# Fixed address phases for the operands of split fp32 matmuls in a two-layer decoder trunk

## The chip, the cores and the metric

The kernel runs on one core of a Trainium2 chip. The metric is the device time of one execution in microseconds (us), the median of several runs. The span of the profiled execution, from its first to its last instruction, is a little shorter than its device time.

## The reference

The reference computes a causal decoder trunk of two layers on one sequence of 256 tokens with 2,048 features, all in float32. Cut to what matters:

```python
for i in range(DEPTH):                       # 2 layers
    xn = rms_norm(x, norm_mix[i])
    y = nsa_mixer(xn, ...) if i % 2 == 0 else mlstm_mixer(xn, ...)
    x = x + y
    x = x + conv_glu_ffn(rms_norm(x, norm_ffn[i]), ...)
return rms_norm(x, norm_final)

def conv_glu_ffn(xn, w_up, conv_w, conv_b, w_down):
    u = xn @ w_up                            # 2048 -> 2 * 5632
    c = causal_conv_width_3(u, conv_w) + conv_b
    gate, val = c[..., :D_FF], c[..., D_FF:]
    return (silu(gate) * val) @ w_down       # 5632 -> 2048
```

The first mixer projects x to queries, keys, values and gates, attends over compressed blocks, selected blocks and a window, and projects back. The second is a matrix memory in chunks (mLSTM), with its own projections in and out. Most of the arithmetic lies in the dense projections: 2,048 by 11,264 up and 5,632 by 2,048 down in each layer, and the mixers' projections in and out.

## The kernel before

Every dense projection is made from split operands. A float32 tensor is held as two tensors of type fp32r, a high half and the rest, and a product is the sum of three matmuls: high by high, high by rest, rest by high. The weights come from HBM in pieces of 512 KB (`load_split`). SyncE's queue loads a piece into `raw` (four buffers), ACT copies it to the high half `whi` (line 188), DVE subtracts to get `wlo` (line 190); each of these has five buffers, used in turn. The activations' halves are `xh` and `xl` for the normed residual stream, `oh` and `ol` for what a mixer puts out (`moh` and `mol` in the second), and `gh` and `gl` for the gated FFN activations.

There are two kinds of product. A column product (`cols_times`, `cols_piece`, lines 224, 226, 227) gives 256 output features for all 256 tokens: weights are stationary (128 by 128), and a row of `xh` or `xl` moves (256 columns). For one contraction step kt there are six matmuls, three for each of two blocks of 128 features; four steps use one weight buffer, and 16 steps, 96 matmuls, make one product. Queries, keys, and the whole FFN up projection are made so. A row product (`rows_mm`, lines 196 to 198) gives 128 tokens by up to 512 features: a block of `xh`, `gh` or `oh` is stationary, and the weights move. `project_out` makes the out and down projections so, 12 matmuls of 512 columns for one weight buffer and one contraction step.

The order of the work is written out by hand. The FFN alternates an up stage of eight column products with a down stage. What follows a product on ACT and DVE is queued (`evacs`, `side`) and issued between weight pieces, so that TensorE always has the next piece's matmuls behind the present ones.

The tiles of a pool lie one behind another in each partition. The pools `const`, `main`, `wpool` and `small` come first, and each stage's pools after them. Before the change three kinds of tile are made longer than their contents by a constant, eight float32 elements, 32 bytes:

```python
SKEW = 8
xh = main.tile([P, KT, S + SKEW], F32R, name="xh")[:, :, :S]
hi = wpool.tile([P, 1024 + SKEW], F32R, name=nm("whi"), tag="whi", bufs=SPB)
gh = wk.tile([P, 8, S + SKEW], F32R, name=nm("gh"), tag="gh")[:, :, :S]
```

In the text, an operand's phase is its address in the partition modulo 256 bytes. `h`, the residual stream, starts at phase 32 and is 16,384 bytes long; `xh` lies behind it, then `xl`, then four buffers of `raw` with 4,096 bytes each, five of `whi`, five of `wlo`.

Of the kernel before, what the change touches and what calls it, by code (L numbers as in the profile page):

```python
# [12 lines left out]
F32 = mybir.dt.float32  # L13
F32R = mybir.dt.float32r
BF16 = mybir.dt.bfloat16
# [6 lines left out]
P = 128  # L22
D = 2048
KT = D // P
S = 256
# [8 lines left out]
EPS = 1e-6  # L34
QSCALE = float(np.float32(128 ** -0.5))
CAP = 15.0
SKEW = 8
NEG = -1e30

C_ID, C_MQ, C_MT, C_CA, C_C1, C_RP = 0, 0, 128, 256, 288, 320  # L40
# [23 lines left out]
def trunk(ctx: ExitStack, tc: tile.TileContext, x, positions, nsa_w_in, nsa_gate_b, nsa_cmp_pe,  # L64
# [3 lines left out]
    nc = tc.nc  # L68
# [4 lines left out]
    const = ctx.enter_context(tc.tile_pool(name="const", bufs=1))  # L73
    main = ctx.enter_context(tc.tile_pool(name="main", bufs=1))
    wpool = ctx.enter_context(tc.tile_pool(name="wpool", bufs=1))
    small = ctx.enter_context(tc.tile_pool(name="small", bufs=2))
    psum = ctx.enter_context(tc.tile_pool(name="psum", bufs=8, space=PSUM))

# [2 lines left out]
    def nm(s):  # L81
        uid[0] += 1
        return f"{s}_{uid[0]}"
# [4 lines left out]
    def fview(t):  # L88
        return t.bitcast(F32)

    h = main.tile([P, NT, D], F32, name="h")
    xh = main.tile([P, KT, S + SKEW], F32R, name="xh")[:, :, :S]
    xl = main.tile([P, KT, S + SKEW], F32R, name="xl")[:, :, :S]

    def load_x(pc):
        for t in range(NT):
# [18 lines left out]
    cst = const.tile([P, C_N - P], F32, name="cst")  # L115
# [1 line left out]

    ident_b = const.tile([P, P], BF16, name="ident_b")
    nc.gpsimd.tensor_copy(ident_b, ident)
    mq_b = const.tile([P, 2, P], BF16, name="mq_b")  # L120
    for b in range(2):
        nc.gpsimd.tensor_copy(mq_b[:, b, :], cst[:, C_MQ:C_MQ + P])
    mt_b = const.tile([P, 2, P], BF16, name="mt_b")
    for b in range(2):
        nc.gpsimd.tensor_copy(mt_b[:, b, :], cst[:, C_MT:C_MT + P])
    sel_b = const.tile([96, MH], BF16, name="sel_b")
    nc.gpsimd.tensor_copy(sel_b, cst[:96, C_SEL:C_SEL + MH])

# [16 lines left out]
    RAWB, SPB, PTB = 4, 5, 4  # L145
# [24 lines left out]
    def queued(engine):  # L170
        return tc.issue_after(fence[engine]) if engine in fence else nullcontext()
# [3 lines left out]
    def preload(w, k0, nk, c0, n):  # L175
        ready[w.tensor.name, w.offset, k0, c0] = load_split(w, k0, nk, c0, n)

    def load_split(w, k0, nk, c0, n):
        got = ready.pop((w.tensor.name, w.offset, k0, c0), None)
        if got is not None:  # L180
            return got
        view = lambda t: t[:, :nk * n].rearrange("p (k c) -> p k c", k=nk)
        raw = wpool.tile([P, 1024], F32, name=nm("raw"), tag="raw", bufs=RAWB)
        nc.sync.dma_start(view(raw), w[k0 * P:(k0 + nk) * P, c0:c0 + n].rearrange("(k p) c -> p k c", p=P))
        hi = wpool.tile([P, 1024 + SKEW], F32R, name=nm("whi"), tag="whi", bufs=SPB)
        lo = wpool.tile([P, 1024 + SKEW], F32R, name=nm("wlo"), tag="wlo", bufs=SPB)
        with queued("act"):
            latest["act"] = act(view(hi), view(raw), AF.Copy).ins  # L188
        with queued("ve"):
            latest["ve"] = ve.tensor_sub(view(lo), view(raw), fview(view(hi))).ins  # L190
        return view(hi), view(lo)
# [8 lines left out]
    def rows_times(w, c0, n, nk):  # L200
        accs = [bank() for _ in range(NT)]
        for k0 in range(0, KT, nk):
            m = min(nk, KT - k0)
            hi, lo = load_split(w, k0, m, c0, n)
            run_hooks()
            for i in range(m):
                kt = k0 + i
                for t in range(NT):
                    rows_mm(hi, lo, i, xh, xl, kt, t, accs[t][:, :n], 0, n, kt == 0, kt == KT - 1)
            tick()  # L210
        return accs
# [19 lines left out]
    def cols_times(w, c0):  # L231
        ps = pair_bank()
        for k0 in range(0, KT, 4):
            cols_piece(ps, w, c0, k0, 4)
        return ps
# [109 lines left out]
    def nsa(norm, nxt):  # L345
        with tc.tile_pool(name="nsa", bufs=1) as pool, tc.tile_pool(name="nsw", bufs=2) as wk:
# [55 lines left out]
            def rope(dst, src):  # L402
                shp = [32, 2, S]
                sw = wk.tile(shp, F32, name=nm("sw"), tag="sw", bufs=1)
                ve.stream_shuffle(sw, src, swap)
                ve.tensor_mul(sw, sw, sin[:, None, :].to_broadcast(shp))
                ve.tensor_mul(dst, src, cos[:, None, :].to_broadcast(shp))
                ve.tensor_add(dst, dst, sw)
# [91 lines left out]

            def q_out(pair, ps):
                qu = wk.tile([P, 2, S], F32, name=nm("qu"), tag="qu", bufs=3)
                qr = wk.tile([P, 2, S], F32, name=nm("qr"), tag="qr", bufs=2)
                ve.tensor_mul(qu, ps, rq[:, None, :].to_broadcast([P, 2, S]))
                act(qr, qu, AF.Copy)
                rope(qr[:32], qu[:32])
                q[pair] = (qu, qr)
# [158 lines left out]
            for pair in range(8):  # L666
                ps = cols_times(w, pair * 256)
                if pair == 1:
                    drain()
                    side.append(lambda: None)  # L670
                    side.extend(attention())
                evacs.append(partial(q_out, pair, ps))
            project_out(nsa_w_out[0], oh, ol, HEADS, nxt, gate_kt=12)

    def mlstm(norm, nxt):
        with tc.tile_pool(name="mls", bufs=1) as pool, tc.tile_pool(name="mlw", bufs=2) as wk:
# [4 lines left out]
            sog = pool.tile([P, NT, D], F32, name="sog")  # L681
            v1 = pool.tile([P, NT, MH, DV + 1], F32, name="v1")
            nc.gpsimd.memset(v1[:, :, :, DV:DV + 1], 1.0)
            oh = pool.tile([P, KT, S], F32R, name="moh")
            ol = pool.tile([P, KT, S], F32R, name="mol")
            gp = pool.tile([P, NT, 2 * MH], F32, name="gp")
# [164 lines left out]

    def ffn(layer, norm, nxt):
        with tc.tile_pool(name=f"ffn{layer}", bufs=1) as pool, tc.tile_pool(name=f"ffw{layer}", bufs=2) as wk:
            wu, wd = ffn_w_up[layer], ffn_w_down[layer]
            taps = tapc[:, layer]

            def conv(ff, tag, ps):
                uu = wk.tile([P, 2, S], F32, name=nm("u"), tag="u" + tag)
                ve.tensor_mul(uu, ps, norm.rbc2)  # L859
                ac = wk.tile([P, 2, S], F32, name=nm("ac"), tag="ac" + tag)  # L860
                for j in range(2):
                    f = ff + j
                    act(ac[:, j, :], uu[:, j, :], AF.Identity, bias=taps[:, 3, f:f + 1],  # L863
                        scale=taps[:, 2, f:f + 1])
                    ve.scalar_tensor_tensor(ac[:, j, 1:], uu[:, j, :S - 1], taps[:, 1, f:f + 1],  # L865
                                            ac[:, j, 1:], op0=ALU.mult, op1=ALU.add)
                    ve.scalar_tensor_tensor(ac[:, j, 2:], uu[:, j, :S - 2], taps[:, 0, f:f + 1],  # L867
                                            ac[:, j, 2:], op0=ALU.mult, op1=ALU.add)
                return ac

            groups = [list(range(0, 4))] + [list(range(f, f + 8)) for f in range(4, NFF, 8)]

            def up(ffs):
                gh = wk.tile([P, 8, S + SKEW], F32R, name=nm("gh"), tag="gh")[:, :, :S]
                gl = wk.tile([P, 8, S + SKEW], F32R, name=nm("gl"), tag="gl")[:, :, :S]
                for i in range(0, len(ffs), 2):
                    res = {}

                    def gate_out(ff, ps, res):
                        res["g"] = conv(ff, "g", ps)  # L880
                        act(res["g"], res["g"], AF.Silu)

                    def val_out(ff, ps, res, i):
                        va = conv(NFF + ff, "v", ps)
                        ve.tensor_mul(va, res["g"], va)
                        act(gh[:, i:i + 2, :], va, AF.Copy)
                        ve.tensor_sub(gl[:, i:i + 2, :], va, fview(gh[:, i:i + 2, :]))

                    evacs.append(partial(gate_out, ffs[i], cols_times(wu, ffs[i] * P), res))
                    evacs.append(partial(val_out, ffs[i], cols_times(wu, (NFF + ffs[i]) * P), res, i))  # L890
                return gh, gl

            def down(ffs, g, norm):
                n = len(ffs)
                project_out(wd[ffs[0] * P:(ffs[0] + n) * P, :], g[0], g[1], n, norm)

            prev = None
            for ffs in groups:
                g = up(ffs)
                if prev is not None:  # L900
                    down(*prev, None)
                prev = (ffs, g)
            down(*prev, nxt)
# [61 lines left out]
    after(12, n0.settle)  # L965
    nsa(n0, n1)
    ffn(0, n1, n2)
    mlstm(n2, n3)
    nf.load()
    ffn(1, n3, nf)  # L970


# [21 lines left out]
```

## Time and profile before

| | us |
|---|---|
| median of 3 runs | 2237.59 |
| lowest and highest run | 2236.51, 2238.47 |
| the profiled execution's own time | 2237.13 |
| its span | 2235.4 |

The profile of that execution has a page (busy times, slices of the span, the chain of work that ended last, costliest groups) and views of the trace: waits, busy time by stage (windows) and instructions in order of time (timeline). In the timeline the first number is a matmul's start and the second its duration. Matmuls overlap, so the difference between two starts is what one adds to the time. Starts are printed to 0.01 us; where the text gives a mean over many matmuls, it is from the trace's starts in whole nanoseconds.

### The profile page before, as it was taken

What the parts mean: (1) busy time and instruction counts of PE and PEld (TensorE: products, weight loads), DVE (VectorE), ACT (ScalarE), POOL (GpSimd) and SP (SyncE); (2) the same over time, 40 slices, a digit from 0 to 9 for tenths busy, and PEclk for the clock granted to TensorE, in tenths of its full rate; (3) what the DMA queues carried; (4) which work ended last, traced back from release to release, by engine and by line L of the source; (5) the groups of instructions that cost most, each with busy time, mean ns of one, the idle gap of its engine ahead of it and who ended that gap; (6) DMA issues with size and microseconds to landing.
All of it is one profiled execution on the core that took longest, in us unless ns stands there. A gap on an engine that the chain in (4) does not pass through costs nothing.

```text
span 2235.4 us, 37288 instructions
## 1 busy us (share of the span) xinstructions
PE 2218.7 (99%) x15072; PEld 2045.1 (91%) x15072; DVE 1442.9 (65%) x2191; ACT 1115.1 (50%) x1565; POOL 19.7 (1%) x58
## 2 busy tenths in 40 slices
PE   9999999999999999999999999999999999999998
PEld 8898789999999899998899988899999898998986
DVE  6487757666666566565645666667666566665755
ACT  6366655544545454454654444555545454454543
POOL 2000000000000000000000000000000000000000
PEclk9999999999999999999999999999999999999999
DMA  8753345666666666666567555566666666665664
GB/s 240 211 158 112 104 161 180 188 187 188 184 189 187 188 189 185 190 184 189 162 187 199 170 169 169 170 197 190 184 187 187 189 189 187 187 184 188 188 188 133
DMA packets 298317, 403.33 MB, mean 180 GB/s; under 512 B 12904, under 2 KB 256840, under 8 KB 298016
## 3 DMA queue, kind: packets, MB, share of 16 engines
q1 hardware_dynamic: 297264, 399.03, 59.0%
q8 instruction: 118, 1.93, 0.4%
q0 software_dynamic: 688, 1.83, 0.2%
q14 instruction: 55, 0.45, 0.1%
q10 hardware_dynamic: 192, 0.08, 0.0%
HBM read 398.80 MB, written 2.10 MB: 179 GB/s over the span
## 4 chain that ended last, share of the span: by engine, by line
PE 96%; DMA 1%; ACT 1%; DVE 1%; issue 0%; SPq 0%; ACTq 0%
PE bank L227 18%; PE bank L224 18%; PE bank L226 18%; PE bank L198 13%; PE bank L196 13%; PE bank L197 13%; DMA raw<-in_nsa_w_in_dram 1%; PE bank L547 1%; PE bank L258 1%; ACT pr L551 1%; ACT whi L188 0%; DVE wlo L190 0%; PE bank L578 0%; DMA h<-in_x_dram 0%; PE bank L522 0%
## 5 line engine op out<-in xcount | busy, mean ns | idle before, releaser
L190 DVE TENSOR_TENSOR wlo<-raw,whi 128x1024 fp32r<-128x1024 f32 (+3 forms) x755 | 911.9, 1209 | 626.5 <-ACT whi L188 624.1
L188 ACT ACTIVATE whi<-raw 128x1024 fp32r<-128x1024 f32 (+3 forms) x755 | 791.4, 1050 | 968.9 <-PE bank L226 501.6
L224 PE MATMUL bank<-xh,whi 128*128 128x256 f32 x3456 | 973.1, 282 | 2.1 <-ACT whi L188 1.4
L227 PE MATMUL bank<-xh,wlo 128*128 128x256 f32 x3456 | 971.2, 281 | 1.5 <-DVE wlo L190 1.5
L226 PE MATMUL bank<-xl,whi 128*128 128x256 f32 x3456 | 969.6, 281 | 0.1
L224 PEld LDWEIGHTS bank<-xh,whi 128*128 128x128 f32 x3456 | 651.1, 188 | 6.6 <-ACT whi L188 2.3
L227 PEld LDWEIGHTS bank<-xh,wlo 128*128 128x128 f32 x3456 | 650.7, 188 | 1.9 <-DVE wlo L190 1.9
L226 PEld LDWEIGHTS bank<-xl,whi 128*128 128x128 f32 x3456 | 650.6, 188 | 1.3 <-DVE xl L264 0.4
L196 PE MATMUL bank<-whi,gh 128*128 128x512 f32 (+1 forms) x712 | 279.2, 392 | 0.0
L198 PE MATMUL bank<-whi,gl 128*128 128x512 f32 (+1 forms) x712 | 278.6, 391 | 0.0
L197 PE MATMUL bank<-wlo,gh 128*128 128x512 f32 (+1 forms) x712 | 278.0, 390 | 0.0
L198 PEld LDWEIGHTS bank<-whi,gl 128*128 128x128 f32 x712 | 133.6, 188 | 30.8
L197 PEld LDWEIGHTS bank<-wlo,gh 128*128 128x128 f32 x712 | 133.7, 188 | 30.2
L196 PEld LDWEIGHTS bank<-whi,gh 128*128 128x128 f32 x712 | 133.6, 188 | 29.6
L196 PE MATMUL bank<-whi,xh 128*128 128x412 f32 (+4 forms) x352 | 128.1, 364 | 0.0
L198 PE MATMUL bank<-whi,xl 128*128 128x412 f32 (+4 forms) x352 | 125.0, 355 | 0.0
L197 PE MATMUL bank<-wlo,xh 128*128 128x412 f32 (+4 forms) x352 | 125.0, 355 | 0.0
L863 ACT ACTIVATE ac<-u,tapc 128x256 f32<-128x256 f32 x176 | 95.0, 587 | 3.8 <-DVE u L859 3.8
L309 DVE TENSOR_TENSOR h<-bank,h 128x512 f32<-128x512 f32 (+1 forms) x113 | 72.8, 679 | 36.9 <-PE bank L198 36.9
L859 DVE TENSOR_TENSOR u<-bank,rbc 128x512 f32<-128x512 f32 x88 | 60.8, 691 | 53.3 <-PE bank L227 53.3
L865 DVE SCALAR_TENSOR_TENSOR ac<-u,tapc,ac 128x255 f32<-128x255 f32 x176 | 77.2, 478 | 3.0 <-ACT ac L863 3.0
L867 DVE SCALAR_TENSOR_TENSOR ac<-u,tapc,ac 128x254 f32<-128x254 f32 x176 | 77.0, 477 | 0.3
(251 smaller groups left out, 1509.0 us busy)
## 6 DMA issues: line engine op xcount, KB each, us to landing
raw<-in_ffn_w_up_dram SPq DMA_DIRECT2D x352, 512.0 KB, 3.7
raw<-in_ffn_w_down_dram SPq DMA_DIRECT2D x176, 512.0 KB, 4.4
raw<-in_mlstm_w_in_dram SPq DMA_DIRECT2D x64, 512.0 KB, 3.8
raw<-in_nsa_w_in_dram SPq DMA_DIRECT2D x51, 512.0 KB, 4.4
raw<-in_nsa_w_out_dram SPq DMA_DIRECT2D x32, 512.0 KB, 3.7
raw<-in_mlstm_w_out_dram SPq DMA_DIRECT2D x32, 512.0 KB, 4.0
raw<-in_mlstm_w_in_dram SPq DMA_DIRECT2D x32, 412.0 KB, 4.0
raw<-in_nsa_cmp_w_dram SPq DMA_DIRECT2D x16, 256.0 KB, 3.4
```

Of the source, the lines that this page charges most:

```text
L188: latest["act"] = act(view(hi), view(raw), AF.Copy).ins
L190: latest["ve"] = ve.tensor_sub(view(lo), view(raw), fview(view(hi))).ins
L196: mm(o, a, hi[:, i, c:e], start=first, stop=False)
L197: mm(o, a, lo[:, i, c:e], start=False, stop=False)
L198: mm(o, b, hi[:, i, c:e], start=False, stop=last)
L224: mm(ps[:, j, :], a, xh[:, kt, :], start=(kt == 0 and j == 0), stop=False, skip_group_check=True)
L226: mm(ps[:, j, :], a, xl[:, kt, :], start=False, stop=False, skip_group_check=True)
L227: mm(ps[:, j, :], b, xh[:, kt, :], start=False, stop=(kt == KT - 1 and j == 1), skip_group_check=True)
L309: ve.tensor_add(h[:, t, a:b], acc[:, :b - a], h[:, t, a:b])
L863: act(ac[:, j, :], uu[:, j, :], AF.Identity, bias=taps[:, 3, f:f + 1], scale=taps[:, 2, f:f + 1])
L865: ve.scalar_tensor_tensor(ac[:, j, 1:], uu[:, j, :S - 1], taps[:, 1, f:f + 1], ac[:, j, 1:], op0=ALU.mult, op1=ALU.add)
L867: ve.scalar_tensor_tensor(ac[:, j, 2:], uu[:, j, :S - 2], taps[:, 0, f:f + 1], ac[:, j, 2:], op0=ALU.mult, op1=ALU.add)
```

## The change

The extra 32 bytes are dropped from `xh`, `xl`, `whi`, `wlo`, `gh` and `gl`, so their rows and buffers are whole multiples of 256 bytes. Small unused tiles (`pad_x`, `pad_w`, `pad_m`, `pad_f0` and `pad_f1`, of 64 or 192 bytes) are put ahead of them and set the phase at which each family starts. Two mask tiles are held once and broadcast instead of twice, and `qr`, the roped queries of the attention, gets a third buffer.

```diff
-SKEW = 8
@@ trunk
     wpool = ctx.enter_context(tc.tile_pool(name="wpool", bufs=1))
+    wpool.tile([P, 48], F32, name="pad_w")
...
     h = main.tile([P, NT, D], F32, name="h")
-    xh = main.tile([P, KT, S + SKEW], F32R, name="xh")[:, :, :S]
-    xl = main.tile([P, KT, S + SKEW], F32R, name="xl")[:, :, :S]
+    main.tile([P, 16], F32, name="pad_x")
+    xh = main.tile([P, KT, S], F32R, name="xh")
+    xl = main.tile([P, KT, S], F32R, name="xl")
...
-    mq_b = const.tile([P, 2, P], BF16, name="mq_b")
-    for b in range(2):
-        nc.gpsimd.tensor_copy(mq_b[:, b, :], cst[:, C_MQ:C_MQ + P])
+    mq_1 = const.tile([P, P], BF16, name="mq_b")
+    nc.gpsimd.tensor_copy(mq_1, cst[:, C_MQ:C_MQ + P])
+    mq_b = mq_1[:, None, :].to_broadcast([P, 2, P])
...
@@ load_split
-        hi = wpool.tile([P, 1024 + SKEW], F32R, name=nm("whi"), tag="whi", bufs=SPB)
-        lo = wpool.tile([P, 1024 + SKEW], F32R, name=nm("wlo"), tag="wlo", bufs=SPB)
+        hi = wpool.tile([P, 1024], F32R, name=nm("whi"), tag="whi", bufs=SPB)
+        lo = wpool.tile([P, 1024], F32R, name=nm("wlo"), tag="wlo", bufs=SPB)
@@ nsa, q_out
-                qr = wk.tile([P, 2, S], F32, name=nm("qr"), tag="qr", bufs=2)
+                qr = wk.tile([P, 2, S], F32, name=nm("qr"), tag="qr", bufs=3)
@@ mlstm
+            pool.tile([P, 16], F32, name="pad_m")
             oh = pool.tile([P, KT, S], F32R, name="moh")
@@ ffn
+            pool.tile([P, 48], F32, name=f"pad_f{layer}")
...
-                gh = wk.tile([P, 8, S + SKEW], F32R, name=nm("gh"), tag="gh")[:, :, :S]
-                gl = wk.tile([P, 8, S + SKEW], F32R, name=nm("gl"), tag="gl")[:, :, :S]
+                gh = wk.tile([P, 8, S], F32R, name=nm("gh"), tag="gh")
+                gl = wk.tile([P, 8, S], F32R, name=nm("gl"), tag="gl")
```

`mt_b` is changed as `mq_b` is.

## Rows read from the trace of the kernel before

**Rows 1.** The page: busy time of the engines, and the chain that ended last.

```profile
PE 2218.7 (99%) x15072; PEld 2045.1 (91%) x15072; DVE 1442.9 (65%) x2191; ACT 1115.1 (50%) x1565; POOL 19.7 (1%) x58
...
PE 96%; DMA 1%; ACT 1%; DVE 1%; issue 0%; SPq 0%; ACTq 0%
```

**Rows 2.** The page's costliest groups: busy us, mean ns, then idle us before.

```profile
L224 PE MATMUL bank<-xh,whi 128*128 128x256 f32 x3456 | 973.1, 282 | 2.1 <-ACT whi L188 1.4
L227 PE MATMUL bank<-xh,wlo 128*128 128x256 f32 x3456 | 971.2, 281 | 1.5 <-DVE wlo L190 1.5
L226 PE MATMUL bank<-xl,whi 128*128 128x256 f32 x3456 | 969.6, 281 | 0.1
```

**Rows 3.** Waits of TensorE, longest in total first: us, times, longest.

```profile
PE bank L227 <- DVE wlo L190: 1.5, 2, 0.8
```

**Rows 4.** Windows of a down and an up stage: engines by busy us, clock.

```profile
599.14:643.62 44.48, 44.48 (x194) 36.03 (x193) 26.04 (x29) 18.60 (x19) 0.00 (x0) 1.00 0.63 190
643.62:734.27 90.65, 90.65 (x769) 90.65 (x768) 60.34 (x76) 45.31 (x53) 0.00 (x0) 1.00 0.62 187
```

**Rows 5.** Timeline: the first matmuls of these stages and of the next.

```profile
599.14 0.39 PE L196 MATMUL bank<-whi,gh 128*128 128x512 f32 x1
...
643.62 0.27 PE L224 MATMUL bank<-xh,whi 128*128 128x256 f32 x1
...
734.27 0.39 PE L196 MATMUL bank<-whi,gh 128*128 128x512 f32 x1
```

**Rows 6.** Timeline of the attention: a bf16 matmul of 256 columns, and its successor.

```profile
151.18 0.27 PE L548 MATMUL bank<-mq_b,ident_b 128*128 128x256 bf16 x1
151.29 0.59 PE L547 MATMUL bank<-kr,qr 128*128 128x512 f32 x1
```

**Rows 7.** Timeline: kt steps at activation phase 96, weight buffer 0, first and last.

```profile
90.07 0.28 PE L224 MATMUL bank<-xh,whi 128*128 128x256 f32 x1
90.19 0.28 PE L226 MATMUL bank<-xl,whi 128*128 128x256 f32 x1
90.30 0.28 PE L227 MATMUL bank<-xh,wlo 128*128 128x256 f32 x1
90.42 0.28 PE L224 MATMUL bank<-xh,whi 128*128 128x256 f32 x1
90.53 0.28 PE L226 MATMUL bank<-xl,whi 128*128 128x256 f32 x1
...
90.77 0.28 PE L224 MATMUL bank<-xh,whi 128*128 128x256 f32 x1
...
2116.05 0.28 PE L224 MATMUL bank<-xh,whi 128*128 128x256 f32 x1
...
2116.74 0.28 PE L224 MATMUL bank<-xh,whi 128*128 128x256 f32 x1
```

**Rows 8.** Timeline: kt steps at activation phase 224, weight buffer 1, first and last.

```profile
23.25 0.28 PE L224 MATMUL bank<-xh,whi 128*128 128x256 f32 x1
...
23.98 0.28 PE L224 MATMUL bank<-xh,whi 128*128 128x256 f32 x1
...
2113.20 0.28 PE L224 MATMUL bank<-xh,whi 128*128 128x256 f32 x1
...
2113.93 0.28 PE L224 MATMUL bank<-xh,whi 128*128 128x256 f32 x1
```

**Rows 9.** Timeline: down-projection steps at stationary phase 32, weight buffer 0, first and last.

```profile
1037.94 0.39 PE L196 MATMUL bank<-whi,gh 128*128 128x512 f32 x1
...
1040.73 0.39 PE L196 MATMUL bank<-whi,gh 128*128 128x512 f32 x1
...
2170.63 0.39 PE L196 MATMUL bank<-whi,gh 128*128 128x512 f32 x1
...
2173.41 0.39 PE L196 MATMUL bank<-whi,gh 128*128 128x512 f32 x1
```

**Rows 10.** The instructions on `qr`: what ACT's copy sat idle for (us, times).

```profile
  PE bank L547: 2.7, 3
```

More of the change, by code (lines that the diff above doesn't have):

```diff
@@ L119, in trunk @@
     nc.gpsimd.tensor_copy(ident_b, ident)
-    mq_b = const.tile([P, 2, P], BF16, name="mq_b")
-    for b in range(2):
-        nc.gpsimd.tensor_copy(mq_b[:, b, :], cst[:, C_MQ:C_MQ + P])
-    mt_b = const.tile([P, 2, P], BF16, name="mt_b")
-    for b in range(2):
-        nc.gpsimd.tensor_copy(mt_b[:, b, :], cst[:, C_MT:C_MT + P])
+    mq_1 = const.tile([P, P], BF16, name="mq_b")
+    nc.gpsimd.tensor_copy(mq_1, cst[:, C_MQ:C_MQ + P])
+    mq_b = mq_1[:, None, :].to_broadcast([P, 2, P])
+    mt_1 = const.tile([P, P], BF16, name="mt_b")
+    nc.gpsimd.tensor_copy(mt_1, cst[:, C_MT:C_MT + P])
+    mt_b = mt_1[:, None, :].to_broadcast([P, 2, P])
     sel_b = const.tile([96, MH], BF16, name="sel_b")
```

## Prediction

> **What bounds the kernel now.** I read the page first: TensorE is busy for 99% of the span, and 96% of the chain that ended last is TensorE [rows 1]. The reader should then ask whether those matmuls wait for anything. They don't: the costliest matmul lines have 2.1, 1.5 and 0.1 us of idle time before them in 2,235 us [rows 2], and the longest entry of the waits is 1.5 us [rows 3]. So the time is the number of matmuls times the distance from one start to the next, and only a change of that distance can pay. A matmul's own duration (282 ns) is no price, because neighbours overlap; the distance is.
>
> The windows by stage give the distance. In an up projection, 768 matmuls of 256 columns start between 643.62 and 734.27 us [rows 4, 5]: 90.65 / 768 = 118.0 ns each. In a down projection, 192 matmuls of 512 columns take 599.14 to 643.62 [rows 4, 5]: 44.48 / 192 = 231.7 ns. The granted clock is 1.00 in both, the 2.4 GHz level, at which 256 columns are 106.7 ns of cycles. A bf16 matmul of 256 columns in the attention needs 109 ns from its start to the next (151.18 to 151.29) [rows 6]. So each split fp32r matmul carries some 9 ns that a bf16 one doesn't. In the up stage the weight-load row PEld is busy for all 90.65 us [rows 4]: the next stationary operand is always being loaded while the present one is multiplied.
>
> Is the 9 ns the same everywhere? No, and that is the point of the case. Adding up the tiles' bytes in the order of allocation gives every operand's address mod 256, its phase. Rows of `xh` and `xl` are 1,056 bytes (4 x 256 + 32), so the phase is 32 + 32·kt. The five weight buffers are 4,128 bytes apart, so `whi` stands at 32, 64, 96, 128, 160 and `wlo` at 192, 224, 0, 32, 64. One kt step is six matmuls with one activation phase and one weight buffer, and there are 8 x 5 = 40 such pairings. At activation 96 and buffer 0 (32 and 192) the six took 0.70 us in the first of 44 cases and 0.69 in the last [rows 7]; over the 44 the mean is 698.1 ns, 116.4 a matmul. At activation 224 and buffer 1 (64 and 224) they took 0.73 us in the first and in the last [rows 8]; mean of 44: 725.5 ns, 120.9 a matmul. The 40 means lie between 116.2 and 120.9, their average is 118.1, and within one phase context of four neighbouring matmuls the starts scatter by only 1.0 ns. The phases set the distance; the kernel now visits all 40 pairings in turn and pays their average.
>
> **The change, part by part.** *Column products (lines 224, 226, 227).* There are 3,456 of each [rows 2], 10,368 in all. After the change `pad_x` puts `xh` and `xl` at 96 (32 + 64) and, with rows of 1,024 bytes, keeps them there; `pad_w` puts `whi` and `wlo` at 32 (96 + 192 = 288), and 4,096-byte buffers keep them there. Thus every matmul has activation 96 and weight 32. The nearest pairing of the old trace is the one of rows 7; only its `wlo` stood elsewhere (192). Inside it, with activation 96 on both sides, the mean distances are 113.8 ns where weight 32 is followed by weight 32 (line 224 to 226, 90.42 to 90.53), 115.3 for 32 to 192 (226 to 227, 90.19 to 90.30) and 118.3 for 192 to 32 (227 to 224, 90.30 to 90.42) [rows 7]. Their mean is 115.8. What one matmul loses can move its neighbour's start, so the single 113.8 is not safe to take alone, and the mean of the three still has a third of its loads at 192. An additive fit over the 10,191 undisturbed distances, with terms for the phases of the neighbours, gives 115.8 to 117.3 for 96 and 32 throughout in its better-fitting forms. I take 116.0. Bounds: 113.8 below, 118.3 above; a floor in principle is the 109 of rows 6. (118.1 − 116.0) x 10,368 = 21.8 us saved.
>
> *Down and out projections (lines 196 to 198).* Here weights move (phase 32 from now on) and `oh`, `ol`, `gh`, `gl` are stationary, at 32 through `pad_m`, `pad_f` and the smaller pools. 2,856 matmuls of 512 columns are of this kind. The nearest class, buffer 0 with a stationary phase of 32, has five kt steps of 12 matmuls: 1037.94 to 1040.73 in the first, 2170.63 to 2173.41 in the last [rows 9], mean 232.15 ns a matmul. All 184 such steps average 231.7; their classes run from 230.0 to 233.9. I take +0.4 x 2,856 = +1.1 us, bounds −4.9 and +6.3. The 384 512-wide products on `xh` (stationary 96) I leave at zero; the 412- to 416-wide ones have row pitches that are no multiple of 256, and keep mixed phases.
>
> *The rest.* `qr` gets a third buffer. ACT waited 2.7 us in all for the matmuls that still read the second [rows 10], TensorE not at all: nothing, and with the cover gone at most 2.7 us. Two fewer casts on POOL run at the start, while TensorE waits for x. The broadcast masks change no count of columns. The removed bytes only make room.
>
> *Does anything else catch up?* A 2% faster TensorE asks DVE for 60.3 us in 89.1 instead of 90.65, ACT for 45.3, and DMA for 190 GB/s instead of 187 [rows 4]. All have slack, so the saving should reach the end. The 192 column products fed by the first loads may hide 0.4 us of it.
>
> **A rule against it.** Rows 7 and 8 show the same instructions at 116.4 and 120.9 ns. The Trainium skill ("TensorE: Matmul & The Clock Gate", section "Step-by-step: what each phase is for") says that TensorE has two independent read ports, so that loading the next weights takes nothing from the running matmul. By that rule addresses can't matter, the sum is 0 and the time stays at 2,237 us. This trace differs, by 4.5 ns between two pairings.
>
> **The rivals.** *Nothing gained (0.12).* The spread could be a shift of starts among neighbours whose average every pairing pays; then the distance stays at 117.7 to 118.5 and the time at 2,233 to 2,241. For it: 192 to 32 alone costs 118.3. Against: a shift among neighbours would cancel over six matmuls, and the six still differ by 27 ns.
>
> *Slower through a fixed collision (0.09).* Rotating phases are an insurance: now a bad pairing is paid at 2 of 40 places, afterwards it would be paid 10,368 times. If 96 against 32 with `wlo` at 32 too behaves as rows 8, the price is (120.9 − 118.1) x 10,368 = +29 us, 2,266 us. It decides from 118.5 on. For it: 32/32 was never seen, since `wlo` always stood 160 beyond `whi`. Against: of the 40 pairings the one nearest is the second fastest.
>
> *A larger gain (0.23).* The only distance with exactly the new phases on both sides is 113.8. If that holds throughout, 4.3 x 10,368 = 44.6 us go, and with the projections' +1.1 the time is 2,194.
>
> *The forecast (0.56)*: 115 to 117.6 ns, which is 2,206 to 2,233 us.
>
> **How the numbers follow.** The profiled execution took 2,237.13 us (span 2,235.4 and 1.7 around it), 0.5 us from the runs' median of 2,237.59, so no correction is due. 2,237.1 − 21.8 + 1.1 = 2,216.4 us. The range reaches down to the larger gain, 2,194, and up to 2,236, into the case of no change; about 2 in 10 lie outside, most of it above. The outer bounds together would be 2,237.1 − 44.6 − 4.9 = 2,187.6 and 2,237.1 + 2.1 + 6.3 = 2,245.5. Within 0.2%, about what a measurement here tells from no change, is ±4.5 us, a distance of 117.7 to 118.5. Faster 0.80, same 0.11, slower 0.09.
>
> **What the profile will show.** Right: up stages of 768 matmuls shrink from 90.65 to near 89.1 us, with every kt step alike instead of 0.69 to 0.73; down stages stay near 44.5. TensorE's waits stay at a few us. Wrong: up stages at 90.6 (no gain) or above 91, down stages above 45, or waits of TensorE for `whi` and `wlo` that grow as the matmuls get shorter.

## The result, and the profile after

The changed kernel takes 2221.94 us (four runs, 2221.16 to 2222.85) against 2238.03 us before in the same runs: ratio 0.9932, 95% interval 0.9918 to 0.9945. The forecast was 2216.4. The size is close and the reason is not: the column products, forecast to give 21.8 us, gave about 3, and the row products, forecast to cost 1.1 us, gave 13.

The page after: busy time, then the column products' groups (lines are one further on; columns as in [rows 2]).

```profile
PE 2203.8 (99%) x15072; PEld 2042.1 (92%) x15072; DVE 1444.2 (65%) x2191; ACT 1113.4 (50%) x1565; POOL 19.1 (1%) x56
...
L225 PE MATMUL bank<-xh,whi 128*128 128x256 f32 x3456 | 970.4, 281 | 3.2 <-ACT whi L189 2.6
L228 PE MATMUL bank<-xh,wlo 128*128 128x256 f32 x3456 | 965.8, 280 | 1.5 <-DVE wlo L191 1.5
L227 PE MATMUL bank<-xl,whi 128*128 128x256 f32 x3456 | 965.4, 279 | 0.1
```

TensorE still waits for next to nothing: 3.2, 1.5 and 0.1 us ahead of these lines in the whole run. The windows of the same down and up stage after (us and count of PE, PEld, DVE, ACT, POOL; clock; DMA; GB/s):

```profile
596.60:640.15 43.55, 43.55 (x194) 36.05 (x193) 26.01 (x29) 18.60 (x19) 0.00 (x0) 1.00 0.64 192
640.15:730.61 90.46, 90.46 (x770) 90.45 (x768) 60.42 (x76) 45.25 (x53) 0.00 (x0) 1.00 0.61 187
```

Against [rows 4] the down stage is 0.93 us shorter (192 matmuls, 231.7 to 226.8 ns each) and the up stage 0.19 us (768 matmuls, 118.0 to 117.8). The regularity came as forecast. The timeline after, the first matmul of a kt step in the up stage and of the next step:

```profile
644.75 0.28 PE L225 MATMUL bank<-xh,whi 128*128 128x256 f32 x1
...
645.46 0.28 PE L225 MATMUL bank<-xh,whi 128*128 128x256 f32 x1
```

The six take 0.71 us, here and in the following steps; [rows 7, 8] had 0.69 to 0.73. Over the trace the column distances have a mean of 117.8 ns and a standard deviation of 0.7 (before: 118.1 and 2.5). The sum by kind: columns (118.09 − 117.78) x 10,368 = 3.2 us; row products on `oh`, `gh`, `moh`, 231.7 to 227.2 ns, 4.5 x 2,856 = 12.9 us; the 384 on `xh` lose (231.7 to 233.2) 0.6 us. That is a gain of 15.5 us, while the span is 14.8 us shorter; the compression matmuls of the first mixer took 1.5 us longer from start to start, and shares of a microsecond lie elsewhere.

### The profile page after: what moved, and what is told of

Its sections match the earlier page's. It is cut to its first block, busy times and chain, and to the rows that moved or that the text cites. A ratio compares the mean times of both kernels' runs of the same rounds, so it can differ in the third digit from the quotient of the medians.

```text
span 2220.6 us, 37284 instructions
## 1 busy us (share of the span) xinstructions
PE 2203.8 (99%) x15072; PEld 2042.1 (92%) x15072; DVE 1444.2 (65%) x2191; ACT 1113.4 (50%) x1565; POOL 19.1 (1%) x56
## 4 chain that ended last, share of the span: by engine, by line
PE 97%; DMA 1%; ACT 1%; DVE 1%; issue 0%; SPq 0%; ACTq 0%
PE bank L225 18%; PE bank L228 18%; PE bank L227 18%; PE bank L197 13%; PE bank L199 13%; PE bank L198 13%; DMA raw<-in_nsa_w_in_dram 1%; PE bank L548 1%; PE bank L259 1%; PE bank L579 0%; DMA h<-in_x_dram 0%; ACT whi L189 0%; ACT pr L552 0%; PE bank L523 0%; DVE wlo L191 0%; PE bank L597 0%
```

## Experiments

All start from the changed kernel. `pad(pool, bytes)` is an unused tile of that size. Times are medians; "before" ran in the same job.

**Which pairs are fast.** Two runs, of one execution each, cut every activation tensor into four groups of rows with phases of their own (a helper class `Phased` returns the row kt from its group).

```diff
-    xh = main.tile([P, KT, S], F32R, name="xh")
+    xh = Phased(main, KT, (0, 32, 64, 128), name="xh")       # second run: (160, 192, 224, 0)
...
-            oh = pool.tile([P, HEADS, S], F32R, name="oh")
+            oh = Phased(pool, HEADS, (0, 64, 96, 128), name="oh")   # (32, 160, 192, 224); moh, gh too
```

First run: 

> The changed kernel with weights at phase 32, but each activation tensor cut into four groups of rows at phases of their own: xh and xl at 0, 32, 64, 128 for four kt steps each; oh, ol, moh, mol, gh, gl at 0, 64, 96, 128. qr has two buffers here, to make room. Pairing theory (the fixed pair of phases sets the distance of two matmuls, and 96 against 32 happens to be an average pair for column products): the four column groups differ by at least 3 ns, between 113 and 122; the equal phases (32) are near 113, since row products gained 4.7 ns at equal phases. Row products at stationary 96 repeat the 233.3 ns that xh as a stationary operand showed at 96, and differ by 3 ns or more from the 227 of equal phases. Rival (any fixed pair gives the same, the phases only shift starts among neighbours; the row products gained by rows and buffers that are whole multiples of 256 bytes): column groups all within 117.3 to 118.3, row groups all within 226.5 to 228.5.

Second run: 

> As the run before, with xh and xl at 160, 192, 224, 0 and the stationary outputs at 32, 160, 192, 224. Pairing theory: again a spread of 3 ns or more among the column groups, the group at 0 equal to that of the run before within 0.5 ns, the row groups at 32 at 227 and the others elsewhere. Rival: all column groups within 117.3 to 118.3, all row groups within 226.5 to 228.5.

Measured, mean distance in ns by phase, weights at 32 (96 for columns is the changed kernel; the others alternate with three more phases, 24 matmuls each):

| phase of the activation | 0 | 32 | 64 | 96 | 128 | 160 | 192 | 224 |
|---|---|---|---|---|---|---|---|---|
| columns, activation moves | 118.3 | 119.4 | 117.7 | 117.8 | 119.9 | 118.8 | 117.5 | 113.9 |
| rows, `oh`/`gh`/`moh` stationary | 233.2 | 228.5 | 233.1 | 233.4 | 234.0 | 232.8 | 233.4 | 229.5 |

One run took 2249.98 us, the other 2224.79. The timeline of a column product in the second run, at the first matmul of each group (160, 192, 224, 0) and of the next product:

```profile
427.44 0.28 PE L248 MATMUL bank<-xh,whi 128*128 128x256 f32 x1
...
430.29 0.28 PE L248 MATMUL bank<-xh,whi 128*128 128x256 f32 x1
...
433.11 0.28 PE L248 MATMUL bank<-xh,whi 128*128 128x256 f32 x1
...
435.84 0.28 PE L248 MATMUL bank<-xh,whi 128*128 128x256 f32 x1
...
438.67 0.28 PE L248 MATMUL bank<-xh,whi 128*128 128x256 f32 x1
```

24 matmuls take 2.85, 2.82, 2.73 and 2.83 us. The pairing theory stands, though one detail of it fell: equal phases are fast for rows and slow for columns. In these runs 96 is an ordinary phase for columns and 224 the outlier; for rows 32 and 224 are fast, the other six alike. The rival is out. That a column's phase alone fixes its distance does not follow, and the runs further on show otherwise.

**The pairing that the prediction rested on**, restored by moving `wlo` alone:

```diff
+        pad(wpool, 160)          # once, between the rings: whi at 32, wlo at 192
         lo = wpool.tile([P, 1024], F32R, name=nm("wlo"), tag="wlo", bufs=SPB)
```

> The changed kernel with one pad more, so that wlo stands at phase 192 while whi stays at 32 and the activations at 96: the pairing of the old trace on which the prediction rested, now throughout. Pairing theory: column products at the mean of the three old distances, 115.8 ns, instead of 117.8, that is 20 us less; row products, with wlo moving at 192 over a stationary 32, at the 232.2 ns of the old class instead of 227.2, 14 us more; together about 2216 us. Rival (any fixed pair gives the same): columns 117.8, rows 227, 2222 us.

Measured 2217.48 us, ratio 0.9908 (0.9893 to 0.9922). Windows of the same two stages:

```profile
593.02:637.61 44.59, 44.59 (x194) 36.00 (x193) 26.04 (x29) 18.58 (x19) 0.00 (x0) 1.00 0.61 191
637.61:726.37 88.76, 88.76 (x770) 88.75 (x768) 60.25 (x76) 45.33 (x53) 0.00 (x0) 1.00 0.62 190
```

The up stage gains (115.6 ns each) and the down stage loses (232.2), as the old classes said. Over the trace the three column distances are 113.9, 115.4 and 118.3 ns, the ones read from [rows 7] to 0.1. The rows were read rightly; they do not describe `wlo` at 32. The 113.9 is the distance of two matmuls at 96 against 32, the pair that took 117.8 in the changed kernel: the two runs differ in the phase of `wlo`, the third weight load of each group of three matmuls, and in nothing else.

**Stationary outputs at 96.**

```diff
+            pad(pool, 64)            # oh, ol at 96; moh, mol, gh, gl likewise
             oh = pool.tile([P, HEADS, S], F32R, name="oh")
```

> The changed kernel with oh, ol, moh, mol, gh, gl at phase 96 instead of 32; weights stay at 32, activations at 96. Pairing theory: the 2,856 row products with these stationary operands go from 227.2 to the 233.3 ns that xh showed at 96: 17 us more, 2239 us. Rival (whole multiples of 256 bytes are what helped, whatever the phase): 2222 us, rows at 227.

Measured 2238.24 us, ratio 1.0001 (0.9991 to 1.0011): the whole gain is gone. The down stage:

```profile
596.98:641.79 44.81, 44.81 (x195) 36.10 (x194) 26.07 (x29) 18.62 (x19) 0.00 (x0) 1.00 0.63 190
```

233.4 ns a matmul, while the up stage stayed at 90.45 us. Rows and buffers of whole 256 bytes are worth nothing by themselves; the pair 32 and 32 is.

**Activations at 224.**

```diff
-    main.tile([P, 16], F32, name="pad_x")
+    pad(main, 192)      # and 64 bytes instead of 192 ahead of raw
```

> The changed kernel with xh and xl at phase 224 instead of 96, nothing else. Pairing theory, by the groups of the two mapping runs: column products 113.9 ns instead of 117.8 (10,368 of them: -40 us), the 384 row products with xh stationary 229.3 instead of 233.2 (-1.5 us): 2180 us. Rival (the group at 224 was fast only through its neighbours at other phases in the mixed run): 117.5 or so, 2220 us.

Measured 2206.91 us, ratio 0.9864 (0.9849 to 0.9879): faster, by much less than 42 us. The first up stage of the first layer (its last 1,008 matmuls), and the second (768):

```profile
362.30:476.64 114.34, 114.34 (x1012) 114.34 (x1010) 82.54 (x108) 63.07 (x76) 0.00 (x0) 1.00 0.65 195
498.41:588.87 90.46, 90.46 (x770) 90.45 (x769) 60.40 (x76) 45.26 (x53) 0.00 (x0) 1.00 0.61 186
```

113.4 ns each in one, 117.8 in the other, with equal phases, matmuls and clock. Neither theory had this. The timeline of the two starts (lines 248, 250, 251 are the column product here, 222 a row product):

```profile
361.94 0.61 PE L304 MATMUL bank<-ident,rstd 128*128 128x128 f32 x4
362.30 0.37 PE L248 MATMUL bank<-xh,whi 128*128 128x256 f32 x1
362.50 0.28 PE L250 MATMUL bank<-xl,whi 128*128 128x256 f32 x1
362.62 0.28 PE L251 MATMUL bank<-xh,wlo 128*128 128x256 f32 x1
362.74 0.28 PE L248 MATMUL bank<-xh,whi 128*128 128x256 f32 x1
362.85 0.28 PE L250 MATMUL bank<-xl,whi 128*128 128x256 f32 x1
362.96 0.28 PE L251 MATMUL bank<-xh,wlo 128*128 128x256 f32 x1
...
498.19 0.39 PE L222 MATMUL bank<-whi,gl 128*128 128x512 f32 x1
498.41 0.28 PE L248 MATMUL bank<-xh,whi 128*128 128x256 f32 x1
498.53 0.28 PE L250 MATMUL bank<-xl,whi 128*128 128x256 f32 x1
498.65 0.28 PE L251 MATMUL bank<-xh,wlo 128*128 128x256 f32 x1
498.76 0.28 PE L248 MATMUL bank<-xh,whi 128*128 128x256 f32 x1
498.88 0.28 PE L250 MATMUL bank<-xl,whi 128*128 128x256 f32 x1
```

The first stream begins with a distance of 0.20 us and is at 0.11 from its fourth matmul on; the second is at 0.12 from its first. Each of these two steady distances is called a level from here on. The level is fixed within a few matmuls of a stage's start and holds for up to 1,008 of them; no stage lies between the two levels. All eight up stages that start right behind a row product are at 117.8; both whose long stream starts behind the four small matmuls of line 304, which broadcast the norm's factors, are at 113.4.

**The same differences, 128 bytes on.**

```diff
+    pad(wpool, 64)      # xh at 96 as before, whi and wlo at 160; oh, moh, gh at 160
```

> Weights and stationary outputs at 160 instead of 32, activations left at 96: the differences between the operands are those of the run with activations at 224, every address is 128 bytes further on modulo 256. If only the difference of two phases counts: the same 113.9 and 227.2 ns, 2180 us. If absolute phases count (the old trace's pairings with equal differences still differed by up to 4 ns): another pair of distances; columns anywhere from 114 to 120 ns, 2180 to 2245 us.

Measured 2215.24 us, ratio 0.9899 (0.9885 to 0.9912). Rows: 227.1 ns on `oh`, `gh`, `moh` and 229.3 on `xh`, against 227.1 and 229.6 at 224. Columns: the same two levels, 113.3 and 117.8, but all ten long up stages took the upper one and only short stretches, of at most 144 matmuls, the lower. A long up stage and a short stretch of the second mixer (144 matmuls):

```profile
363.47:482.28 118.81, 118.81 (x1012) 118.81 (x1010) 82.95 (x108) 63.05 (x76) 0.00 (x0) 1.00 0.62 189
1256.18:1272.60 16.42, 16.42 (x147) 16.42 (x146) 8.93 (x9) 6.89 (x8) 0.00 (x0) 1.00 0.73 216
```

For this one shift of all phases, by 128 bytes, the differences between them set the distances, and which level is taken is a second matter; other shifts were not run.

**A finer grid.** Weights at 32, `Phased` with (208, 216, 232, 240) for `xh`, `xl` and (16, 24, 40, 48) for the stationary outputs.

> A mapping run on a finer grid around the best pairs: weights at 32, xh and xl in four groups at 208, 216, 232, 240, stationary outputs in four groups at 16, 24, 40, 48; qr has two buffers. If the good pairing is a slot 32 bytes wide (addresses count in lines of 32 bytes or more): 232 and 240 as fast as 224 (113.9), 208 and 216 like 192 (117.5); row groups 40 and 48 like 32 (227 to 228.5), 16 and 24 like 0 (233). If distances change byte by byte: values between those of the neighbours, or lower than 113.9.

Measured 2251.51 us. Columns: 119.2, 120.1, 120.5, 119.0 ns; rows: 227.8, 233.3, 230.6, 233.2. Neither reading holds: 8 bytes from 224 the gain is lost, and 16 bytes below 32 rows are still fast, while 8 bytes below they are not. No slot 32 bytes wide shows in this one execution, and nothing beats 113.9 in it.

**The third `qr` buffer.**

```diff
-                qr = wk.tile([P, 2, S], F32, name=nm("qr"), tag="qr", bufs=3)
+                qr = wk.tile([P, 2, S], F32, name=nm("qr"), tag="qr", bufs=2)
```

> The changed kernel with two qr buffers as before the change; all phases unchanged. Prediction's step: the third buffer is worth nothing (TensorE never waited for it): 2222 us within 0.2%. Rival: it carried part of the gain, 2.7 us (the ACT waits of the old trace) or more: 2225 us.

Measured 2224.15 us, ratio 0.9937 (0.9924 to 0.9949): no difference from the changed kernel (0.9932) that can be told. ACT's 2.7 us wait of [rows 10] came back, and nothing else.

**What chooses the level.** What TensorE ran just before a stream is called its entry here. Activations at 224, and fp32 transposes into the bank that the next product overwrites:

```diff
     def cols_times(w, c0):
         ps = pair_bank()
+        if after_row_product:                  # eight up stages
+            for _ in range(n % 4 + 1):         # n: running number of the stage
+                nc.tensor.transpose(ps[:, 0, :P], ident, ident)
```

> The kernel with activations at 224, in which column products ran at either 113.3 or 117.8 ns for a whole stage, with equal phases: at 117.8 in all eight up stages that begin right behind a row product, at 113.3 in most stretches that begin behind transposes. Here those eight stages begin with 1, 2, 3, 4 fp32 transposes (the same in both layers) into the bank that the first product then overwrites. Entry theory (the first few matmuls set a timing that the stage then keeps): at least some of the stages go to 113.3, each of those saving 768 x 4.5 = 3.4 us less 0.3 for its transposes; if all do, 25 us less, 2182 us. Rival (the level depends on the stage, by what DVE, ACT and DMA do meanwhile, not on the entry): all eight stay at 117.8 and the time at 2208 us.

Measured 2195.24 us, ratio 0.9811 (0.9797 to 0.9826). The four stages of the first layer, behind one, two, three, four transposes:

```profile
499.09:589.63 90.54, 90.54 (x771) 90.54 (x769) 60.37 (x76) 45.25 (x53) 0.00 (x0) 1.00 0.61 186
633.29:723.83 90.54, 90.54 (x772) 90.54 (x771) 60.25 (x76) 45.28 (x53) 0.00 (x0) 1.00 0.61 186
767.62:854.76 87.14, 87.14 (x771) 87.14 (x770) 59.86 (x76) 45.27 (x53) 0.00 (x0) 1.00 0.63 193
898.65:985.81 87.16, 87.16 (x772) 87.16 (x770) 59.76 (x76) 45.17 (x53) 0.00 (x0) 1.00 0.63 193
```

Three and four bring the lower level, one and two don't; the second layer's stages repeat it to 0.01 us. Two runs ask whether 96 has the lower level too, with two transposes, and with three or four in turn:

> The changed kernel (activations at 96) with two fp32 transposes ahead of each of the eight up stages. If the two levels exist at any pair of phases: some stages fall to 113.3 here as well, up to 25 us less, 2197 us. If 96 against 32 holds only the level of 117.8 (its stretches behind transposes ran at 117.8 too, but for some dozen matmuls): 2222 us and up to 3 us for the transposes.

> The changed kernel (activations at 96) with three or four fp32 transposes, in turn, ahead of each of the eight up stages. If 96 against 32 has the level of 113.3 too, and one or two transposes only failed to reach it as they did at 224: all eight stages fall, 2197 us. If it has not: 117.8 in all stages, 2222 to 2225 us.

Measured 2223.59 us (ratio 0.9939, 0.9923 to 0.9956) and 2225.06 us (0.9946, 0.9929 to 0.9963). All eight up stages stay at 90.54 us in both. The pair of 96 and 32 has the lower level all the same. In the first of the two runs one column product of the first mixer, behind the compression matmuls, reaches it. The windows of that product, from its fourth matmul to its last, and of an up stage of the same run:

```profile
96.70:107.13 10.43, 10.43 (x94) 10.43 (x93) 9.34 (x13) 4.37 (x5) 0.00 (x0) 1.00 0.83 252
639.20:729.74 90.54, 90.54 (x771) 90.54 (x770) 60.30 (x76) 45.29 (x53) 0.00 (x0) 1.00 0.61 186
```

10.43 / 92 = 113.4 ns a matmul in the product, 90.54 / 768 = 117.9 in the stage. So at 96 none of the entries with transposes brought a stage to the lower level, but it is not barred to this pair.

**Three transposes everywhere**, activations at 224:

```diff
+        if after_row_product:                  # all 15 such products
+            for _ in range(3):
```

> Activations at 224, weights and stationary outputs at 32, and three fp32 transposes ahead of each of the 15 column products that follow a row product (three and four brought an up stage to 113.3 ns in both layers, one and two did not). Entry theory: all eight later up stages at 113.3 ns, four of them 3.4 us faster each than in the run with one to four transposes (2195.2), the mixers' products 1 us more: about 2181 us. Rival (the stage's place decides, and stages three and four happened to take the fast level): the first and second stage stay at 117.8, 2195 us.

Measured 2192.59 us, ratio 0.9800 (0.9785 to 0.9814), the fastest here, yet 11 us short. The first three up stages:

```profile
363.04:481.85 118.81, 118.81 (x1012) 118.81 (x1011) 82.95 (x108) 63.03 (x76) 0.00 (x0) 1.00 0.62 189
503.88:591.01 87.13, 87.13 (x771) 87.13 (x770) 59.86 (x76) 45.29 (x53) 0.00 (x0) 1.00 0.64 192
634.80:721.94 87.14, 87.14 (x771) 87.14 (x770) 59.86 (x76) 45.28 (x53) 0.00 (x0) 1.00 0.63 193
```

The eight stages fell to 113.5 ns as the entry theory says. But the first stage of each layer went from 114.34 to 118.81 us, 8.9 us in both layers together, and its 1,008 matmuls begin behind the same four small matmuls as before (line 304 there, 310 here). What differs is the stretch of 120 column matmuls ahead of those four, with activations at 224 alone and in this run:

```profile
347.72:361.94 14.22, 14.22 (x124) 14.22 (x123) 10.49 (x24) 7.96 (x12) 0.20 (x4) 1.00 0.76 231
```

```profile
348.98:362.68 13.70, 13.70 (x123) 13.70 (x122) 10.44 (x24) 8.06 (x12) 0.20 (x4) 1.00 0.76 229
```

That is 118.5 and 114.2 ns a matmul, the long first distance included. The first is at the upper level and the stage behind it at the lower; the second is at the lower and the stage behind it at the upper. Both layers show it, and so do the run with one to four transposes and the run with all phases 128 bytes on: in eight cases of eight the long stretch takes the level that the 120 did not have. Nor do three transposes always bring the lower level: of the 15 products behind them one, of the second mixer, began with 48 matmuls at 117.8 ns. So the entry theory in the form put on record, that the kind of entry decides, does not hold; what ran before the entry counts too.

## Why the prediction came out right

*TensorE's distances set the time, and phases move the distances*: shown. That the phases of a pair alone set them, as the forecast assumed, is not so for columns: 96 against 32, and 224 against 32, each ran at 113.3 and at 117.8 ns. Moving the stationary outputs by 64 bytes cost 16 us, moving the activations by 128 gave 15, and TensorE was busy for 99% of the span in each. By the rule of the Trainium skill weighed in the prediction ("TensorE: Matmul & The Clock Gate", section "Step-by-step: what each phase is for"), loading the next weights takes nothing from the running matmul. If nothing else counted, all pairs would be alike; in the runs they are not, with 113.9 to 119.9 ns for columns.

*The column term, 21.8 us saved*: failed. It measured 3.2. The step was the transfer from the old pairing, with `wlo` at 192, to 32 throughout: 116.0 ns was taken and 117.8 came. With `wlo` back at 192 the columns were at 115.9, so the reading of [rows 7] as to that pairing was sound and the additive fit was not. One effect of a neighbour's phase doesn't add to another's. [Rows 7] held a sign of it: the prediction calls 113.8 the only distance with the new phases on both sides, but the first two matmuls of the step (90.07 and 90.19) also have 96 against 32, and over the 44 cases they are 117.5 ns apart, close to the 117.8 that came. The rival "nothing gained" described the columns, but its reason, a shift of starts that every pairing pays alike, was wrong: 224 had 113.9 in the mixed run. The 113.8 of the rival "A larger gain" exists at 96 against 32, but no long stage took it.

*The row term, +1.1 us*: failed in sign. It measured −12.9, beyond the bound of −4.9. The same transfer: the class of [rows 9], 232.15 ns, had `wlo` at 192. With `wlo` there again it is 232.3, with `wlo` at 32 it is 227.2.

*Third buffer, slack of DVE, ACT and DMA*: right; the masks have no run of their own, and the sum by kind leaves them nothing. The up stage's DVE time is 60.4 of 90.5 us, and even 87.1 us leave it slack.

The total was right by luck: the two errors, 18.6 us and 14.0 us, nearly cancelled. The bounds were drawn from pairings that contained `wlo` at other phases, so they didn't bound a pairing that had never run.

## What to carry to other kernels

Where TensorE is full and its operands are fp32r, the distance between matmul starts is a quantity to measure for each pair of operand phases; a few row groups with phases of their own map eight pairs in two runs. Such a map shows one distance of each pair; whether the pair has another shows only in long streams of it. Don't extrapolate from a rotating pattern to a fixed one. Look at the distances stage by stage, not at their mean: two levels hidden in a mean are worth more here than the change was.

## What was not expected of the hardware

A stream of 256-column matmuls with equal phases ran at one of two steady distances, 113.3 or 117.8 ns, and kept the one it started with for up to 1,008 matmuls. With activations at 224 three or four fp32 transposes ahead of a stage behind a row product chose the lower, twelve times of twelve. What in the start decides, and why no stage of 96 against 32 took the lower, stays open. The trace gives two signs, at 224. In the 22 stages that begin behind fp32 transposes or the four small matmuls, in the runs with activations at 224, the first distance was 201 ns in the six at the upper level and 205 to 208 ns in the sixteen at the lower. And six short streams right behind a row product (four at 224, two in the run with all phases 128 bytes on) went over to the lower level, all just after one distance of 122 to 125 ns among their first five. So a start that is a few nanoseconds late goes with the lower level there; at 96 first distances of 204 and 205 ns led to the upper. Within a stream the levels differ in the distance and in the weight load's start ahead of its matmul's (110.0 ns at the lower level, 114.4 at the upper with activations at 224, 115.3 at 96). That these come from reads of the two operands meeting in the memory is an argument only; nothing here shows it.
